# A decoder kernel on one core: in products by seven, the cast of the second sums is queued behind ScalarE's copies of the first group's banks

## The chip, the core and the metric

The kernel runs on one core of a Trainium2 chip. Five engines work side by side, each on its own queue in order: TensorE (PE, with its weight loads shown apart as PEld) multiplies matrices into PSUM, VectorE (DVE) and ScalarE (ACT) do elementwise work, GpSimd (POOL) here mostly issues transfers, SyncE (SP) issues the loads of weights. They wait for each other through semaphores. The metric is the device time of one execution in microseconds (us), as the median of several runs. A profiled execution also gives a span, from the first to the last instruction.

## The reference

A decoder trunk of two layers over 512 tokens of width 1024, in float32. Each layer is a SwiGLU FFN at half weight, a mixer (gated linear attention in the first layer, stick-breaking attention in the second), and a second FFN at half weight, each behind an RMSNorm. So four FFNs run:

```python
D_MODEL = 1024; SEQ = 512; DEPTH = 2; D_FF = 2816

def swiglu(h, w_gate, w_up, w_down):
    return (jax.nn.silu(h @ w_gate) * (h @ w_up)) @ w_down

for i in range(DEPTH):
    x = x + 0.5 * swiglu(rmsnorm(x, ffn1_norm[i]), ffn1_w_gate[i], ffn1_w_up[i], ffn1_w_down[i])
    h = rmsnorm(x, mix_norm[i])
    y = gla_mixer(h, ...) if i % N_MIXERS == 0 else sb_mixer(h, ...)
    x = x + y
    x = x + 0.5 * swiglu(rmsnorm(x, ffn2_norm[i]), ffn2_w_gate[i], ffn2_w_up[i], ffn2_w_down[i])
return rmsnorm(x, final_norm)
```

## The kernel before

**Precision.** Every float32 matrix is cut into two parts in a reduced format: `h` is a cast of it (ScalarE, line 138 for weights, 838 for activations) and `l` is what the cast lost (VectorE, lines 139 and 839: the original minus the cast). A product takes three matmuls: high by high, low by high, high by low. So for each piece of weights ScalarE makes `wh`, then VectorE makes `wl`, and only then can TensorE run all three.

**Products by seven.** Most FFN products are computed as a 2 by 2 block product with seven block products in place of eight, in the manner of Winograd and Strassen. A 1024 by 256 chunk of gate or up weights is cut into four blocks; `sums_12` makes the first two sums of blocks (tile `s12`, VectorE, lines 718 and 719), `sums_34` the second two (tile `s34`, lines 724 and 725). The rows of the trace call both tiles `s`. The work is two entries of a queue called the feed:

- `body_1` (line 750): four groups of 12 matmuls. The first writes bank `w` (from block a11). ScalarE then copies `w` to bank `z` (line 761), because both the later groups on `w` and the one on `z` go on from it. The second writes `q` (from `s12`); ScalarE copies it out (765). The third adds to `w` (from `s12`) and so may not begin before the copy at 761 has read `w`; ScalarE copies the result out (769). The fourth adds to `z` (from a2), read by a silu (743) or a VectorE product (746).
- `body_2` (line 776): three groups, on `w` (from `s34`), `q` (from `s34`) and `w` (from a2). The first of them may not begin before `w` was copied at 769. ScalarE copies `w` to `u3` (783), VectorE adds (784, 789), and for gate chunks three silus (743) follow.

The down product of two groups in each FFN does the same in halves (`seven_down`, line 358; matmuls at line 394): the same seven groups, each for two values of m, with two copies to `z` (412) in `body_1`, and with VectorE's additions into the residual x (line 400) in place of the copies at 765 and 769. There `body_2` adds to `w` too, and so it may not begin before the addition at line 400 has read `w`. Its sums are made at lines 378, 379, 385 and 386, and its `u3` is copied at 439.

**What sets the order.** `Feed.start` (line 146) is called when an entry begins. It calls `split` (the casts and subtractions, line 122) for this entry and the ones behind it, three entries at most and as long as no more than four tiles of 1024 columns are cut, so the casts of coming entries are in the program before the matmuls of this one. A scheduler then orders each engine's queue by the program's order and by priority; `ahead()` (line 192) raises the priority of a block. On the chip each queue runs in that order. TensorE's order is that of the program.

**Buffers.** `wh` and `wl` of 1024 columns have four buffers each, those of 512 columns one each; the sums share four.

**Stages of an FFN.** Chunks of 256 columns run in six groups. The first two chunks of gate use ordinary products; then gate and up chunks by seven alternate, with down products between them. Where two pairs of entries by seven stand directly behind one another, `body_2` of the one is followed by `body_1` of the next.

Of the kernel before, what the change touches and what calls it, by code (L numbers as in the profile page):

```python
# [10 lines left out]
F32 = mybir.dt.float32  # L11
F32R = mybir.dt.float32r
# [28 lines left out]
def pair(t):  # L41

    return t.rearrange("p (two n) -> p two n", two=2)
# [3 lines left out]
def decoder(ctx: ExitStack, tc: tile.TileContext, a: dict, out: bass.AP):  # L47
# [60 lines left out]
    class Entry:  # L108
# [3 lines left out]

        def __init__(self, units, body):
            self.units, self.body, self.W, self.views = units, body, None, None

        def view(self):

# [1 line left out]
                self.views = [view(ch.load()) for ch, view, _, _ in self.units]  # L119
            return self.views  # L120

        def split(self):
            if self.W is None:
                self.W = []
                for r, (_, _, n, m) in zip(self.view(), self.units):
                    few = n * m < 1024
                    if few:

                        h, l = (
                            st["few"].tile([P, n * m], F32R, tag="v" + t, bufs=1, name="w" + t) for t in "hl"  # L130
                        )
                    else:
                        h, l = (wp.tile([P, n * m], F32R, tag="w" + t, bufs=4, name="w" + t) for t in "hl")
                    h, l = (t.rearrange("p (n m) -> p n m", m=m) for t in (h, l))
                    pieces = r if isinstance(r, tuple) else (r,)
                    for i, part in enumerate(pieces):
                        k = slice(i * n // len(pieces), (i + 1) * n // len(pieces))
                        st["cut"] = nc.scalar.copy(h[:, k], part).ins  # L138
                        nc.vector.tensor_tensor(out=l[:, k], in0=part, in1=h[:, k].bitcast(F32), op=ALU.subtract)  # L139
                    self.W.append((h, l))  # L140

    class Feed:
        def __init__(self):
# [2 lines left out]
        def start(self):  # L146
            i = self.pos
            self.pos += 1
            used = 0
            for e in self.q[i : i + 3]:  # L150
                used += sum(n * m >= 1024 for _, _, n, m in e.units)
                if used > 4:
                    break
                e.split()
            for e in self.q[i : i + 4]:
                e.view()
            for e in self.q[i : i + 6]:
                for u in e.units:
                    u[0].load()
            e = self.q[i]  # L160
            return e.body(e.W)
# [196 lines left out]
    def seven_down(pool, w, r0, hs, part):  # L358

        H = T // 2
        lower, upper = (
            Chunk(w[r0 : r0 + 4 * P, c : c + 256].rearrange("(f p) c -> p f c", p=P), 4, 256)
            for c in (part * 256, 512 + part * 256)
        )
        lower.few = upper.few = True
        v = {}

        def halves():  # L370

            lo, up = (c.load().rearrange("p (c two) d -> p two c d", two=2) for c in (lower, upper))
            return lo[:, 0], lo[:, 1], up[:, 0], up[:, 1]

        def sums_12(_):
            a11, _, a21, a22 = halves()
            s = v["s12"] = pool().tile([P, 4, 256], F32, tag="s", bufs=4, name="s12")
            nc.vector.tensor_tensor(out=s[:, 0:2], in0=a21, in1=a22, op=ALU.add)
            nc.vector.tensor_tensor(out=s[:, 2:4], in0=s[:, 0:2], in1=a11, op=ALU.subtract)
            return s  # L380

        def sums_34(_):
            a11, a12, a21, _ = halves()
            s = pool().tile([P, 4, 256], F32, tag="s", bufs=4, name="s34")
            nc.vector.tensor_tensor(out=s[:, 0:2], in0=a11, in1=a21, op=ALU.subtract)
            nc.vector.tensor_tensor(out=s[:, 2:4], in0=a12, in1=v["s12"][:, 2:4], op=ALU.subtract)
            return s

        def prod(ps, w, k0, m, b, first):
            for c in range(2):  # L390
                bh, bl = (turns(t) for t in hs[c][b])
                wh, wl = (t[:, k0 + c, m * P : (m + 1) * P] for t in w)
                for n, (l_, r_) in enumerate(((wh, bh), (wl, bh), (wh, bl))):
                    st["pe"] = nc.tensor.matmul(  # L394
                        ps, l_, r_, start=first and c + n == 0, stop=c == 1 and n == 2, skip_group_check=True
                    ).ins

        def add(m, up, col, ps):
            x = pair(xs[part * 2 + m + 4 * up][:, col * H : col * H + H])
            nc.vector.scalar_tensor_tensor(out=x, in0=ps, scalar=0.5, in1=x, op0=ALU.mult, op1=ALU.add)  # L400

        def body_1(W):
            a11, s, v["a2"] = W
            ws, zs, qs = [], [], []
            for m in range(2):
                ws.append(psum("ps_w")[:, 0:H])
                prod(ws[m], a11, 0, m, "b11", True)
            for m in range(2):


                zs.append(psum("ps_z")[:, 0:H])
                nc.scalar.copy(zs[m], ws[m])
            yield

            ps = psum("ps_q")
            for m in range(2):
                qs.append(ps[:, m * H : (m + 1) * H])
                prod(qs[m], s, 0, m, "t1", m == 0)
            for m in range(2):
                add(m, 1, 1, flat(qs[m]))  # L420
            yield
            for m in range(2):
                prod(ws[m], s, 2, m, "t2", False)
                add(m, 0, 1, flat(ws[m]))
            yield
            for m in range(2):
                prod(zs[m], v["a2"], 0, m, "b21", False)
                add(m, 0, 0, flat(zs[m]))
            v["w"], v["q"] = ws, qs
            yield  # L430

        def body_2(W):
            (s,) = W
            ws, qs = v["w"], v["q"]

            u3 = pool().tile([P, 2, H], F32, tag="c", bufs=1, name="u3")
            for m in range(2):
                prod(ws[m], s, 0, m, "t3", False)
                nc.scalar.copy(pair(u3[:, m]), flat(ws[m]))
                add(m, 1, 1, pair(u3[:, m]))  # L440
            yield
            for m in range(2):
                prod(qs[m], s, 2, m, "b22", False)
            for m in range(2):
                add(m, 0, 1, flat(qs[m]))
            yield
            for m in range(2):
                prod(ws[m], v["a2"], 2, m, "t4", False)
                add(m, 1, 0, flat(ws[m]))
            yield  # L450

        units = [(lower, lambda t: halves()[0], 2, 256), (lower, sums_12, 4, 256), (lower, lambda t: halves()[1::2], 4, 256)]
        feed.q.append(Entry(units, body_1))
        feed.q.append(Entry([(lower, sums_34, 4, 256)], body_2))

    def back_tok(w, r0, nf, hs, done):

# [159 lines left out]
    class FFN:  # L617
# [90 lines left out]
        def seven(self, ch, group=None):  # L708
# [41 lines left out]
            def body_1(W):  # L750


                a11, s, a2 = W
                v["a2"] = a2
                v["w"], v["q"] = psum("ps_w"), psum("ps_q")
                z = psum("ps_z")[:, 0:H]
                w, q = (v[n][:, 0:H] for n in "wq")
                o0, o1 = v["o"] = [self.tp.tile([P, T], F32, tag="t", name=n) for n in ("o0", "o1")]
                prod(w, a11, 0, half(0, 0))
                with ahead():  # L760
                    nc.scalar.copy(z, w)  # L761
                yield
                prod(q, s, 0, lambda j: self.t_half(0, j))
                with ahead():
                    nc.scalar.copy(pair(o1[:, H:T]), flat(q))
                yield
                prod(w, s, 4, lambda j: self.t_half(1, j), first=False)
                with ahead():
                    nc.scalar.copy(pair(o0[:, H:T]), flat(w))
                yield  # L770
                prod(z, a2, 0, half(4, 0), first=False)
                with ahead():
                    gate(o0, 0, flat(z))
                yield
# [44 lines left out]
            units = [(ch, lambda t: t[:, 0:4, 0:P], 4, P), (ch, sums_12, KD, P), (ch, lambda t: t[:, 4:8], 4, 256)]  # L819
            feed.q.append(Entry(units, body_1))  # L820
            feed.q.append(Entry([(ch, sums_34, KD, P)], body_2))

        def t_half(self, i, j):

# [57 lines left out]
        def evac_u(self, ps, group):  # L882
            t = self.tp.tile([P, T], F32, tag="t", name="t")
            if not self.normed:
                nc.vector.tensor_tensor(out=pair(t), in0=flat(ps), in1=pair(st["R"]), op=ALU.mult)
            nc.vector.tensor_tensor(
                out=pair(t), in0=flat(ps) if self.normed else pair(t), in1=pair(self.gates.pop(0)), op=ALU.mult
            )
            self.close(t, group)

        def close(self, t, group):
            h = self.hp.tile([P, T], F32R, tag="hh", name="hh")
# [1043 lines left out]
```

## Time and profile before

| | |
|---|---|
| median of 3 runs | 1779.5 us (1779.32 to 1780.22) |
| the profiled execution's own time | 1778.36 us |
| its span | 1776.4 us |
| granted TensorE clock over the span | 0.999 |
| PE busy | 1755.4 us, 99% of the span |
| DVE busy | 1509.6 us, 85% |
| ACT busy | 1079.6 us, 61% |
| matmuls at line 733 and 394 (products by seven), one group of 12 | 1.34 us without a wait |

The profile lists busy time by engine, groups of instructions with their mean time, and who waited for whom. In rows of the timeline the first number is the start in us from the span's beginning, the second the duration in us (of the whole merged row); what stands in brackets is the idle time of that engine before the row, and what ended it. Instructions on one engine overlap a little at their ends, so the distance from one start to the next is what a queue pays.

### The profile page before, as it was taken

What the parts mean: (1) busy time and instruction counts of PE and PEld (TensorE: products, weight loads), DVE (VectorE), ACT (ScalarE), POOL (GpSimd) and SP (SyncE); (2) the same over time, 40 slices, a digit from 0 to 9 for tenths busy, and PEclk for the clock granted to TensorE, in tenths of its full rate; (3) what the DMA queues carried; (4) which work ended last, traced back from release to release, by engine and by line L of the source; (5) the groups of instructions that cost most, each with busy time, mean ns of one, the idle gap of its engine ahead of it and who ended that gap; (6) DMA issues with size and microseconds to landing.
All of it is one profiled execution on the core that took longest, in us unless ns stands there. A gap on an engine that the chain in (4) does not pass through costs nothing.

```text
span 1776.4 us, 31377 instructions
## 1 busy us (share of the span) xinstructions
PE 1755.4 (99%) x12714; PEld 1630.6 (92%) x12714; DVE 1509.6 (85%) x2474; ACT 1079.6 (61%) x1883; POOL 55.6 (3%) x77
## 2 busy tenths in 40 slices
PE   9999999999999999999999999999999999999998
PEld 8999999889888899999889999999888888999997
DVE  8999797786888989888798988967898679997986
ACT  7556556554655566555655555655888755565564
POOL 0000000200000000000000000010000000000000
PEclk9999999999999999999999999999999999999999
DMA  5543435422123433444434344342212234434441
GB/s 167 154 120 119 125 102 148 113 66 73 54 90 100 121 117 120 119 120 125 129 95 133 102 125 126 118 120 83 84 48 72 72 95 131 126 104 123 120 138 52
DMA packets 186388, 193.14 MB, mean 109 GB/s; under 512 B 4930, under 2 KB 171124, under 8 KB 186244
## 3 DMA queue, kind: packets, MB, share of 16 engines
q1 hardware_dynamic: 177760, 175.91, 31.7%
q0 software_dynamic: 8240, 14.95, 4.6%
q8 instruction: 99, 1.62, 0.4%
q14 instruction: 45, 0.37, 0.1%
q10 hardware_dynamic: 244, 0.29, 0.0%
HBM read 175.17 MB, written 2.10 MB: 100 GB/s over the span
## 4 chain that ended last, share of the span: by engine, by line
PE 60%; DVE 30%; ACT 5%; issue 3%; DMA 2%; SPq 0%; DVEq 0%; ACTq 0%
PE ps_w L733 13%; PE ps_d L80 12%; DVE wl L139 9%; PE ps_f L80 7%; PE ps_q L733 6%; PE ps_t L80 4%; PE ps_z L733 3%; PE ps_b L80 3%; PE ps_w L394 3%; ACT wh L138 2%; DVE x L400 2%; DVE hl L839 1%; PE ps_q L394 1%; DVE ts L848 1%; PE ps_z L1424 1%
## 5 line engine op out<-in xcount | busy, mean ns | idle before, releaser
L139 DVE TENSOR_TENSOR wl<-raw,wh 128x1024 fp32r<-128x1024 f32 x241 | 255.5, 1061 | 59.4 <-ACT wh L138 58.8
L138 ACT CAST wh<-raw 128x1024 fp32r<-128x1024 f32 x241 | 221.6, 920 | 77.8 <-PE ps_f L80 22.6
L139 DVE TENSOR_TENSOR wl<-s,wh 128x1024 fp32r<-128x1024 f32 x176 | 214.6, 1219 | 50.7 <-ACT wh L138 50.7
L733 PE MATMUL ps_w<-th,wh 128*128 128x256 f32 x864 | 239.4, 277 | 6.3 <-ACT ps_z L761 6.3
L733 PE MATMUL ps_w<-th,wl 128*128 128x256 f32 x864 | 237.6, 275 | 0.0
L733 PE MATMUL ps_w<-tl,wh 128*128 128x256 f32 x864 | 237.6, 275 | 0.0
L138 ACT CAST wh<-s 128x1024 fp32r<-128x1024 f32 x176 | 184.1, 1046 | 69.6 <-DVE s L719 19.4
L733 PEld LDWEIGHTS ps_w<-th,wh 128*128 128x128 f32 x864 | 165.8, 192 | 9.5 <-ACT ps_z L761 9.4
L80 PE MATMUL ps_f<-xh,wh 128*128 128x512 f32 x432 | 166.4, 386 | 0.0
L733 PEld LDWEIGHTS ps_w<-tl,wh 128*128 128x128 f32 x864 | 165.9, 192 | 0.0
L733 PEld LDWEIGHTS ps_w<-th,wl 128*128 128x128 f32 x864 | 165.8, 192 | 0.0
L80 PE MATMUL ps_f<-xh,wl 128*128 128x512 f32 x432 | 164.2, 380 | 0.5 <-DVE wl L139 0.5
L80 PE MATMUL ps_f<-xl,wh 128*128 128x512 f32 x432 | 163.9, 379 | 0.0
L80 PE MATMUL ps_d<-hl,wh 128*128 128x512 f32 x416 | 158.0, 380 | 1.7 <-DVE hl L839 1.7
L80 PE MATMUL ps_d<-hh,wh 128*128 128x512 f32 x416 | 158.0, 380 | 0.5 <-ACT hh L838 0.5
L80 PE MATMUL ps_d<-hh,wl 128*128 128x512 f32 x416 | 157.7, 379 | 0.0
L139 DVE TENSOR_TENSOR wl<-rawd,wh 128x1024 fp32r<-128x1024 f32 (+1 forms) x100 | 96.1, 964 | 15.8 <-ACT wh L138 15.1
L138 ACT CAST wh<-rawd 128x1024 fp32r<-128x1024 f32 (+1 forms) x100 | 82.9, 845 | 39.4 <-PE ps_d L80 25.6
L345 POOL DMA_DIRECT2D x<-d x53 | 45.8, 888 | 1510.1 <-ACT d L344 832.2
L80 PEld LDWEIGHTS ps_f<-xl,wh 128*128 128x128 f32 x432 | 81.6, 189 | 11.5
L80 PEld LDWEIGHTS ps_f<-xh,wl 128*128 128x128 f32 x432 | 81.7, 189 | 11.3 <-DVE wl L139 0.9
L80 PEld LDWEIGHTS ps_f<-xh,wh 128*128 128x128 f32 x432 | 81.7, 189 | 10.8
(355 smaller groups left out, 5331.4 us busy)
## 6 DMA issues: line engine op xcount, KB each, us to landing
raw<-in_ffn_w_gate_dram SPq DMA_DIRECT2D x43, 1024.0 KB, 5.4
raw<-in_ffn_w_up_dram SPq DMA_DIRECT2D x43, 1024.0 KB, 5.4
rawd<-in_ffn_w_down_dram SPq DMA_DIRECT2D x84, 512.0 KB, 3.8
x<-d POOLq DMA_DIRECT2D x53, 256.0 KB, 4.6
raw<-in_gla_w_in_dram SPq DMA_DIRECT2D x12, 1024.0 KB, 5.4
raw<-in_sb_w_in_dram SPq DMA_DIRECT2D x16, 512.0 KB, 3.7
raw<-in_gla_w_out_dram SPq DMA_DIRECT2D x4, 1024.0 KB, 5.1
raw<-in_sb_w_in_dram SPq DMA_DIRECT2D x4, 1024.0 KB, 5.2
```

The lines of the kernel that those rows point to most:

```text
L80: st["pe"] = nc.tensor.matmul(ps, l, r, start=first, stop=last).ins
L138: st["cut"] = nc.scalar.copy(h[:, k], part).ins
L139: nc.vector.tensor_tensor(out=l[:, k], in0=part, in1=h[:, k].bitcast(F32), op=ALU.subtract)
L345: nc.gpsimd.dma_start(xs[k], d, accum_op=ALU.add)
L394: st["pe"] = nc.tensor.matmul(ps, l_, r_, start=first and c + n == 0, stop=c == 1 and n == 2, skip_group_check=True).ins
L400: nc.vector.scalar_tensor_tensor(out=x, in0=ps, scalar=0.5, in1=x, op0=ALU.mult, op1=ALU.add)
L733: st["pe"] = nc.tensor.matmul(o, l_, r_, start=first and j + n == 0, stop=j == 3 and n == 2, skip_group_check=True).ins
L839: nc.vector.tensor_tensor(out=l, in0=t, in1=h.bitcast(F32), op=ALU.subtract)
L848: nc.vector.tensor_tensor(out=o, in0=p, in1=q, op=ALU.subtract)
L1424: nc.tensor.matmul(o_, l_, r_, start=first, stop=last, skip_group_check=True)
```

## The change

`split` takes an instruction to be queued behind, and its body becomes a function `parts` that cuts one piece. ScalarE's cast is traced under `issue_after`, which puts it behind the given instruction on ScalarE's queue. Both makers of products by seven mark the second entry of a pair; `Feed.start` stops before a second entry whose first group's copy isn't in the program yet if the entry two places ahead of it is a second entry too (so for pairs directly behind one another). That entry is cut in `body_1` of its pair instead, behind the copy of bank `w` to `z` (behind the later of the two copies for the halves of down). The copies at 412 are put under `ahead()`, and so are the product and the cut in `evac_u`.

```diff
@@ class Entry
             self.units, self.body, self.W, self.views = units, body, None, None
+            self.second, self.v = False, None
...
-        def split(self):
+        def split(self, after=None):
             if self.W is None:
                 self.W = []
                 for r, (_, _, n, m) in zip(self.view(), self.units):
...
+                    self.W.append(self.parts(r, n, m, after))
+
+        def parts(self, r, n, m, after):
...
+            for i, part in enumerate(pieces):
+                k = slice(i * n // len(pieces), (i + 1) * n // len(pieces))
+                with tc.issue_after(after) if after is not None else ExitStack():
+                    nc.scalar.copy(h[:, k], part)
+                nc.vector.tensor_tensor(out=l[:, k], in0=part, in1=h[:, k].bitcast(F32), op=ALU.subtract)
+            return h, l
@@ Feed.start
-            for e in self.q[i : i + 3]:
+            for n, e in enumerate(self.q[i : i + 3]):
+                if e.v is not None and "copied" not in e.v and self.q[i + n - 2].second:
+                    break
                 used += sum(n * m >= 1024 for _, _, n, m in e.units)
                 if used > 4:
                     break
@@ seven_down, body_1
-                nc.scalar.copy(zs[m], ws[m])
+                with ahead():
+                    v["copied"] = nc.scalar.copy(zs[m], ws[m]).ins
+            v["second"].split(v["copied"])
             yield
@@ seven_down and FFN.seven, at their ends
+        v["second"] = feed.q[-1]
+        feed.q[-1].second, feed.q[-1].v = True, v
@@ FFN.seven, body_1
                 with ahead():
-                    nc.scalar.copy(z, w)
+                    v["copied"] = nc.scalar.copy(z, w).ins
+                v["second"].split(v["copied"])
                 yield
@@ FFN.evac_u
-            nc.vector.tensor_tensor(
-                out=pair(t), in0=flat(ps) if self.normed else pair(t), in1=pair(self.gates.pop(0)), op=ALU.mult
-            )
-            self.close(t, group)
+            with ahead():
+                nc.vector.tensor_tensor(
+                    out=pair(t), in0=flat(ps) if self.normed else pair(t), in1=pair(self.gates.pop(0)), op=ALU.mult
+                )
+                self.close(t, group)
```

TensorE's and SyncE's rows stand in the same order in both kernels; ScalarE's and VectorE's move in the same four stretches of each of the four FFNs, and one load of GpSimd moves by two places. The rows below are of the first FFN. Names with a number are tiles of sums and outputs (numbers differ a little between the kernels); the changed file's lines lie 5 to 15 further down, so that 143 is the cast of weights (138 before), 144 its subtraction (139), 772 the copy to `z` (761), 777 and 781 the copies of `q` and `w` (765, 769), 754 the silu (743), 420 the copy in the halves of down (412), 407 the addition into x (400), 852 and 853 the cut of activations (838, 839).

The first place is ScalarE where a gate pair ends and an up pair begins. Before (`s_1348` are the second sums of the up pair, `s_1426` the first sums of the pair behind it):

```order
L743 ACTIVATE o_1355<-o_1355 128x256
L138 CAST wh<-s_1348 128x1024
L743 ACTIVATE o_1354<-o_1354 128x256
L743 ACTIVATE o_1355<-ps_w 128x256
L138 CAST wh<-s_1426 128x1024
L761 COPY ps_z<-ps_w 128x256
L138 CAST wh<-rawd 128x512
L765 COPY o_1481<-ps_q 128x256
L769 COPY o_1480<-ps_w 128x256
```

The same place in the changed kernel (`s_1422` is the `s_1426` of before):

```order
L754 ACTIVATE o_1355<-o_1355 128x256
L754 ACTIVATE o_1354<-o_1354 128x256
L754 ACTIVATE o_1355<-ps_w 128x256
L772 COPY ps_z<-ps_w 128x256
L143 CAST wh<-s_1348 128x1024
L143 CAST wh<-rawd 128x512
L777 COPY o_1477<-ps_q 128x256
L143 CAST wh<-s_1422 128x1024
L781 COPY o_1476<-ps_w 128x256
```

Both casts of sums that stood before the copy to `z` stand behind it now, and the second of them stands between the copies of `q` and `w`.

The second place is VectorE a little later, at the halves of down (`s_1474`, now `s_1470`, are its second sums, x_85 and so on parts of the residual). Before:

```order
L139 TENSOR_TENSOR wl<-s_1474,wh 128x1024
L746 TENSOR_TENSOR o_1481<-ps_w,o_1355 128x256
L839 TENSOR_TENSOR hl<-o_1480,hh 128x512
L139 TENSOR_TENSOR wl<-s_1552,wh 128x1024
L839 TENSOR_TENSOR hl<-o_1481,hh 128x512
L400 SCALAR_TENSOR_TENSOR x_85<-ps_q,x_85 128x256
L400 SCALAR_TENSOR_TENSOR x_86<-ps_q,x_86 128x256
L400 SCALAR_TENSOR_TENSOR x_81<-ps_w,x_81 128x256
```

In the changed kernel:

```order
L729 TENSOR_TENSOR s_1684<-raw 128x512
L757 TENSOR_TENSOR o_1477<-ps_w,o_1355 128x256
L853 TENSOR_TENSOR hl<-o_1476,hh 128x512
L730 TENSOR_TENSOR s_1684<-s_1684,raw 128x512
L853 TENSOR_TENSOR hl<-o_1477,hh 128x512
L144 TENSOR_TENSOR wl<-s_1470,wh 128x1024
L407 SCALAR_TENSOR_TENSOR x_85<-ps_q,x_85 128x256
L407 SCALAR_TENSOR_TENSOR x_86<-ps_q,x_86 128x256
L407 SCALAR_TENSOR_TENSOR x_81<-ps_w,x_81 128x256
```

The subtraction for the second sums has moved directly in front of the additions into x, and later first sums (729, 730) have come in between.

The third place is ScalarE where the first up pair of group 1 ends and a gate pair begins (`nh`, `hh` are cuts of activations, `s_866`, now `s_862`, the gate pair's second sums). Before:

```order
L783 COPY u_956<-ps_w 128x256
L838 CAST nh<-o_874 128x256
L138 CAST wh<-s_866 128x1024
L138 CAST wh<-rawd 128x1024
L761 COPY ps_z<-ps_w 128x256
L838 CAST hh<-o_875 128x512
L838 CAST hh<-ts 128x512
L838 CAST nh<-ts 128x256
L765 COPY o_1019<-ps_q 128x256
```

In the changed kernel:

```order
L795 COPY u_952<-ps_w 128x256
L852 CAST nh<-o_870 128x256
L852 CAST nh<-ts 128x256
L852 CAST hh<-o_871 128x512
L852 CAST hh<-ts 128x512
L772 COPY ps_z<-ps_w 128x256
L852 CAST nh<-ts 128x256
L143 CAST wh<-s_862 128x1024
L777 COPY o_1011<-ps_q 128x256
L143 CAST wh<-rawd 128x1024
L781 COPY o_1010<-ps_w 128x256
```

Here the two weight casts have left the place before the copy to `z`, and three casts of activations have come to stand there.

More of the change, by code (lines that the diff above doesn't have):

```diff
@@ L125, in split @@
                 for r, (_, _, n, m) in zip(self.view(), self.units):
[L126 to L130, printed above, removed]
-                        )
[L132 to L140, printed above, removed]
+                    self.W.append(self.parts(r, n, m, after))
+        def parts(self, r, n, m, after):
+            few = n * m < 1024
+            if few:
+                h, l = (
+                    st["few"].tile([P, n * m], F32R, tag="v" + t, bufs=1, name="w" + t) for t in "hl"
+                )
+            else:
+                h, l = (wp.tile([P, n * m], F32R, tag="w" + t, bufs=4, name="w" + t) for t in "hl")
+            h, l = (t.rearrange("p (n m) -> p n m", m=m) for t in (h, l))
+            pieces = r if isinstance(r, tuple) else (r,)
+            for i, part in enumerate(pieces):
[4 more added lines that the diff above has]
+            return h, l
     class Feed:
@@ L821, in seven @@
             feed.q.append(Entry([(ch, sums_34, KD, P)], body_2))
+            v["second"] = feed.q[-1]
+            feed.q[-1].second, feed.q[-1].v = True, v
         def t_half(self, i, j):
@@ L885, in evac_u @@
                 nc.vector.tensor_tensor(out=pair(t), in0=flat(ps), in1=pair(st["R"]), op=ALU.mult)
[L886 to L889 removed]
+            with ahead():
+                nc.vector.tensor_tensor(
+                    out=pair(t), in0=flat(ps) if self.normed else pair(t), in1=pair(self.gates.pop(0)), op=ALU.mult
+                )
+                self.close(t, group)
         def close(self, t, group):
```

## The prediction

> **What bounds the kernel now.** I read the page's busy shares first, then the waits of TensorE, then the groups by line, and last the timeline around the longest and the commonest of those waits.
>
> ```profile
> PE 1755.4 (99%) x12714; PEld 1630.6 (92%) x12714; DVE 1509.6 (85%) x2474; ACT 1079.6 (61%) x1883; POOL 55.6 (3%) x77
> PE ps_w L733 <- ACT ps_z L761: 6.3, 16, 1.1
> PEld ps_w L733 <- ACT ps_z L761: 9.4, 16, 1.3
> PEld ps_w L394 <- ACT ps_z L412: 0.5, 1, 0.5
> ```
>
> TensorE is busy in 99% of the span, so only what it waits for can be won, and nearly half of that is one thing: the third group of a product by seven waits for ScalarE's copy to `z`, 16 times. The commonest form of it, on ScalarE and then on TensorE:
>
> ```profile
> 122.44 0.42 ACT L743 ACTIVATE o<-o 128x256 f32<-128x256 f32 x1 [1.84 <-DVE o L784]
> 122.77 1.03 ACT L138 CAST wh<-s 128x1024 fp32r<-128x1024 f32 x1
> 123.70 0.41 ACT L743 ACTIVATE o<-o 128x256 f32<-128x256 f32 x1
> 124.02 0.37 ACT L743 ACTIVATE o<-ps_w 128x256 f32<-128x256 f32 x1
> 124.28 1.05 ACT L138 CAST wh<-s 128x1024 fp32r<-128x1024 f32 x1
> 125.22 0.38 ACT L761 COPY ps_z<-ps_w 128x256 f32<-128x256 f32 x1
> 125.52 0.63 ACT L138 CAST wh<-rawd 128x512 fp32r<-128x512 f32 x1
> ...
> 125.11 0.28 PE L733 MATMUL ps_q<-th,wl 128*128 128x256 f32 x1
> 125.22 0.28 PE L733 MATMUL ps_q<-tl,wh 128*128 128x256 f32 x1
> 125.66 0.38 PE L733 MATMUL ps_w<-th,wh 128*128 128x256 f32 x1 [0.16 <-ACT ps_z L761]
> 125.87 0.28 PE L733 MATMUL ps_w<-th,wl 128*128 128x256 f32 x1
> ```
>
> Three silus of the pair that ends, late because VectorE's sums were late (1.84 us idle), share the queue with two casts of sums at 0.93 and 0.94 from start to start. So the copy starts at 125.22. TensorE steps at 0.11 us (0.112 over many, so 1.34 for a group of 12); the waiting matmul starts 0.44 behind the last, 0.33 too late, and its successor 0.21 behind it, another 0.10. A wait thus costs the visible delay plus 0.10 for starting again.
>
> **What the change removes.** In pairs directly behind one another both casts leave the place ahead of the copy. The first group on `w` ended where `q` began, 11 steps before 125.22, at 123.99; by the rows below a copy follows such an end by 0.2 to 0.25.
>
> ```profile
> 85.50 0.28 PE L733 MATMUL ps_q<-th,wh 128*128 128x256 f32 x1
> 85.75 0.36 ACT L761 COPY ps_z<-ps_w 128x256 f32<-128x256 f32 x1 [0.35 <-PE ps_w L733]
> 86.02 0.62 ACT L838 CAST hh<-o 128x512 fp32r<-128x512 f32 x1
> 86.54 0.62 ACT L838 CAST hh<-ts 128x512 fp32r<-128x512 f32 x1
> 121.99 0.42 DVE L784 TENSOR_TENSOR o<-u,o 128x256 f32<-128x256 f32 x1
> 122.92 0.42 DVE L789 TENSOR_TENSOR o<-ps_q,o 128x256 f32<-128x256 f32 x1
> ```
>
> The silus may start when VectorE is done, at 122.44 and 123.37, the third 0.32 later; so the copy starts at 124.2 and ends before 124.6, and TensorE wants it at 125.33. The wait here is gone. The order shows the same at every one of the 16, and at the one of line 412. A weight load lasts 0.192 (its group reads 192 ns) at a step of 0.112, so 0.08 of each wait hides under the last load:
>
> ```profile
> L733 PEld LDWEIGHTS ps_w<-th,wh 128*128 128x128 f32 x864 | 165.8, 192 | 9.5 <-ACT ps_z L761 9.4
> ```
>
> Removed: 9.4 + 16 x 0.08 = 10.7, and 0.5 + 0.1 = 0.6 at line 412, together **11.3 us**.
>
> [...]
>
> **What it gives back at the halves of down.** ScalarE's cast of the second sums now starts after the copy (0.30 from start to start at 125.22 and 125.52), at 124.5, and ends at 125.55. VectorE's subtraction for it stands at the same place in VectorE's queue as before, so VectorE, which began it at 123.86, waits until 125.6. These are the steps it then takes:
>
> ```profile
> 132.52 1.22 DVE L139 TENSOR_TENSOR wl<-s,wh 128x1024 fp32r<-128x1024 f32 x1
> 133.66 0.42 DVE L746 TENSOR_TENSOR o<-ps_w,o 128x256 f32<-128x256 f32 x1
> 133.99 0.68 DVE L839 TENSOR_TENSOR hl<-o,hh 128x512 fp32r<-128x512 f32 x1
> 134.59 1.22 DVE L139 TENSOR_TENSOR wl<-s,wh 128x1024 fp32r<-128x1024 f32 x1
> 135.72 0.68 DVE L839 TENSOR_TENSOR hl<-o,hh 128x512 fp32r<-128x512 f32 x1
> 136.33 0.75 DVE L400 SCALAR_TENSOR_TENSOR x<-ps_q,x 128x256 f32<-128x256 f32 x2
> 136.99 0.41 DVE L400 SCALAR_TENSOR_TENSOR x<-ps_w,x 128x256 f32<-128x256 f32 x1
> ...
> 137.82 0.28 PE L394 MATMUL ps_w<-nh,wh 128*128 128x256 f32 x1
> ```
>
> From start to start a subtraction of 1024 columns takes 1.14, an operation on 512 columns 0.60, one on 256 columns 0.33 to 0.34, two additions into x 0.66; one addition lasts 0.41. By the order there stand, from that subtraction to the end of the addition that `body_2` of the halves of down waits for, three of 1024 (3.42), nine of 512 (5.40), six of 256 (2.03), two additions from `q` (0.66) and one from `w` (0.41): 11.9 us, ending at 137.5. The third subtraction waits for its cast besides. That cast stands behind the second copy at line 412, which stands behind a cut `hh`; the sum for this cut ends at 133.6 by the same steps; 0.52 for the cut, 0.30 for the copy and 1.05 for the cast give 135.5, where VectorE arrives at 135.3. So 137.7. TensorE, with no wait, is there nine groups behind 125.33, at 125.33 + 9 x 1.34 = 137.39. In the run shown the addition ended at 137.40 and TensorE came at 137.82: 0.42 to spare, and now 0.35 short with the semaphore's 0.05, plus 0.10 for the restart. That is 0.45 of the 0.43 won. Three such places stand in each FFN (the pair behind each of them: 125, 241 and 270 us in the first), and the spacing inside is fixed by TensorE, so 12 x 0.45 = **5.4 us**. Bounds: none (if VectorE's steps run 3% faster), and 12 x 0.8 = 9.6 if the steps are 3% slower.
>
> **What it gives back elsewhere.** The copy at line 769 now stands behind the cast of the second sums (0.95), of 512 columns (0.52), the copy of `q` (0.27) and the cast of the next first sums (0.95); with the copy to `z` (0.27) and its own 0.37 it ends 3.33 behind the start of the copy to `z`. It must end 5.36 (four groups) behind the pair's start; the copy to `z` normally starts 1.34 + 0.2 behind it. The slack is 0.49, so nothing is lost where the silus are on time, as at 124.2. At the worst place they aren't:
>
> ```profile
> 74.64 0.42 DVE L789 TENSOR_TENSOR o<-ps_q,o 128x256 f32<-128x256 f32 x1
> 75.73 0.36 ACT L743 ACTIVATE o<-ps_w 128x256 f32<-128x256 f32 x1
> ...
> 76.01 0.28 PE L733 MATMUL ps_q<-tl,wh 128*128 128x256 f32 x1
> 77.36 0.38 PE L733 MATMUL ps_w<-th,wh 128*128 128x256 f32 x1 [1.07 <-ACT ps_z L761]
> ```
>
> VectorE ends at 75.06, two silus follow at 0.32 each, and the copy starts at 75.73, which leaves TensorE on time at 76.12 within 0.05 (1.2 won and 0.1). But the pair began at 76.12 - 2.68 = 73.44, the copy at 769 ends at 79.06, and TensorE wants it at 78.80: 0.3 lost. The next copy to `z` there has three cuts of activations ahead of it (third place of the order) where it had two casts that were done early. Counting from VectorE's sums at the steps above I get it 0.4 late, then 0.1 at its copy of `w`. With the restarts that is 1.1 of 1.3. This stretch had such a wait in two FFNs; in the other two it had none and loses some 0.1 to 0.2. Together 2 x 1.1 + 2 x 0.15 = **2.5 us**, between 1 and 4.
>
> **What costs nothing.** The order moves no row for `evac_u`: VectorE's order is the same there, and the priority changes nothing. Transfers keep their order; the load that moves on GpSimd's queue waits on nothing that TensorE needs soon. `wl` of the second sums must be there 0.11 behind the start of `body_2`: cast at 2.9, subtraction done at 4.1 behind the pair's start, 1.3 us of cover; without it each pair would lose what is missing. The instructions and their number stay the same.
>
> **The sum.** 11.3 - 5.4 - 2.5 = 3.4, and 0.2 for delays under 0.1 us that go with the removed waits: 3.6 us off the profiled execution's 1778.36 (span 1776.4, 2.0 around it), so 1774.8 (span 1772.8). The median of the runs shown, 1779.5, lies 1.1 above the profiled one: **1775.9 us**.
>
> **Rivals.**
>
> Clean gain: VectorE has its slack, nothing comes back at line 400 and little at 769. For it: 0.42 to spare there before, and VectorE's idle time. Against: the steps above. 11.3 - 1 = 10.3: 1769.2.
>
> No net change: the losses reach their upper bounds, 9.6 + 2.5 against 11.3: 1780, or 1778 to 1781 with one of them less. For it: the first stretch alone gives back nearly all it wins.
>
> Slower, VectorE as the bound: in the longest of these stretches VectorE has almost nothing left.
>
> ```profile
> 122.00:181.00 59.00, 58.39 (x516) 57.91 (x515) 56.49 (x97) 36.70 (x67) 0.00 (x0) 1.00 0.37 117
> 171.28 1.22 DVE L139 TENSOR_TENSOR wl<-s,wh 128x1024 fp32r<-128x1024 f32 x1 [1.09 <-ACT wh L138]
> ```
>
> Its subtraction of second sums now always waits for a cast that follows TensorE. In the first of these stretches that adds waits of about 1.6, 1.0 and 1.7 us to a queue that waited 2.2, so some 2 us, and, counted likewise, 1.7 in the one from 238 us. If the sums behind it are needed at once, TensorE pays these 3.7 us in each FFN, 14.8 in place of the 5.4: 11.3 - 14.8 - 2.5 = -6, so 1785.5. It decides once VectorE's work of a pair no longer ends within the pair's 9.38 us. Against: 56.49 of 59.00 includes the adds and sums that can be late without anyone waiting. [...]
>
> That the change doesn't do what it says: the order excludes it for the casts, and grants it for `evac_u`.
>
> **How the numbers follow.** Forecast (2 to 5.5 us gained) 0.55, clean gain 0.14, no net change 0.20, slower 0.11. About 0.2% (3.6 us) can be told from no change here: that is the middle of my forecast. Faster by more: 0.31 of the forecast's 0.55 and the clean gain, 0.45. Slower by more: VectorE as the bound, 0.11. Within: the rest, 0.44. The range from 1771 to 1781 takes in the bounds of the two losses one at a time, half of the way to the clean gain and the case of no change.
>
> **What would show it.** Right: the waits for line 761 (772 in the changed file) fall below 3 us; new waits of TensorE for VectorE's addition at line 400 (407), about 12 of them at 0.3 each; a few for the copy at 769 (781), all within 74 to 95 us and its like in the third FFN; VectorE's waits for the casts of sums grow. Wrong: the waits at 761 remain; none at 400, or waits for `wl` of the second sums; a total over 1781, which would mean that VectorE no longer keeps up.

## The result, and the profile after

| | before | changed |
|---|---|---|
| median of the runs, us | 1778.69 (14 runs, 1777.63 to 1780.22) | 1775.05 (14 runs, 1774.33 to 1776.63) |
| profiled execution, us | 1778.36 | 1776.0 |
| its span, us | 1776.4 | 1774.1 |
| TensorE's waits for the copy to `z` (PE / PEld), us | 6.3 / 9.4 | 0.2 / 0.6 |

The changed kernel takes 0.998 of the time before, with a 95% interval of 0.9973 to 0.9987: it is 3.6 us faster. The forecast was 1775.9.

First the changed kernel's page: the busy shares, and the groups that answer to those quoted of before.

```profile
PE 1756.3 (99%) x12714; PEld 1631.8 (92%) x12714; DVE 1505.5 (85%) x2474; ACT 1074.7 (61%) x1883; POOL 55.6 (3%) x77
L144 DVE TENSOR_TENSOR wl<-s,wh 128x1024 fp32r<-128x1024 f32 x176 | 215.2, 1223 | 82.6 <-ACT wh L143 80.2
L744 PEld LDWEIGHTS ps_w<-th,wh 128*128 128x128 f32 x864 | 165.8, 192 | 1.8 <-ACT o L781 0.7
```

The subtraction's row on the page before:

```profile
L139 DVE TENSOR_TENSOR wl<-s,wh 128x1024 fp32r<-128x1024 f32 x176 | 214.6, 1219 | 50.7 <-ACT wh L138 50.7
```

The work is the same in number and in length (1223 ns a subtraction after 1219, 192 ns a weight load). What changed is the idle time behind the bar: the loads of the groups on `w` wait 1.8 us where they waited 9.5, and VectorE waits 80.2 us for the casts of sums, where before it waited 50.7. Most of those 30 us cost nothing, since VectorE is not the bound; the part of them that reaches TensorE shows in the next rows.

Next, TensorE's waits in the changed kernel (line waited at, releaser: us in total, times, longest), first of the matmuls, then of the weight loads.

```profile
PE ps_w L401 <- ACT wh L143: 2.6, 9, 0.3
...
PE ps_w L401 <- DVE x L407: 0.8, 3, 0.3
...
PE ps_w L744 <- ACT ps_z L772: 0.2, 1, 0.2
PEld ps_w L401 <- issue: 5.3, 12, 0.5
...
PEld ps_w L744 <- ACT o L781: 0.7, 3, 0.2
PEld ps_w L744 <- ACT ps_z L772: 0.6, 2, 0.4
```

None of the 16 waits of before is left. The two short ones at line 772 (761 before) stand at 86.35 and 955.04 us, at copies that made nobody wait before the change. New are also 12 waits at line 401, the first matmul of `body_2` in the halves of down, at some 0.3 each on the matmul and 0.44 on its load. The profile names VectorE's addition at 407 for three of them and ScalarE's cast at 143 for nine.

The timeline at the commonest place of before shows the part that was won, on ScalarE and then on TensorE:

```profile
122.21 0.42 ACT L754 ACTIVATE o<-o 128x256 f32<-128x256 f32 x1 [1.90 <-DVE o L796]
123.14 0.42 ACT L754 ACTIVATE o<-o 128x256 f32<-128x256 f32 x1 [0.52 <-DVE o L801]
123.47 0.36 ACT L754 ACTIVATE o<-ps_w 128x256 f32<-128x256 f32 x1
123.91 0.36 ACT L772 COPY ps_z<-ps_w 128x256 f32<-128x256 f32 x1
124.17 1.05 ACT L143 CAST wh<-s 128x1024 fp32r<-128x1024 f32 x1
...
124.93 0.28 PE L744 MATMUL ps_q<-tl,wh 128*128 128x256 f32 x1
125.05 0.28 PE L744 MATMUL ps_w<-th,wh 128*128 128x256 f32 x1
```

The silus start when VectorE is done, with no cast between them; the copy ends at 124.27, the third group begins at 125.05, one step of 0.12 behind the last matmul. The same pair then pays at the halves of down. VectorE, ScalarE and TensorE there:

```profile
135.19 1.22 DVE L144 TENSOR_TENSOR wl<-s,wh 128x1024 fp32r<-128x1024 f32 x1 [0.15 <-ACT wh L143]
136.33 0.75 DVE L407 SCALAR_TENSOR_TENSOR x<-ps_q,x 128x256 f32<-128x256 f32 x2
137.00 0.75 DVE L407 SCALAR_TENSOR_TENSOR x<-ps_w,x 128x256 f32<-128x256 f32 x2
...
134.09 1.06 ACT L143 CAST wh<-s 128x1024 fp32r<-128x1024 f32 x1
...
136.99 0.28 PE L401 MATMUL ps_z<-hl,wh 128*128 128x256 f32 x1
137.56 0.35 PE L401 MATMUL ps_w<-nh,wh 128*128 128x256 f32 x1 [0.29 <-ACT wh L143]
137.74 0.28 PE L401 MATMUL ps_w<-nh,wl 128*128 128x256 f32 x1
```

The first of the two additions from `w` ends at about 137.41 (137.00 and 0.41 for one), and TensorE, which would have come at 137.10, starts at 137.56. The cast that the profile names had ended at 135.15. By the starts, 12 such places are late by 0.43 to 0.45 each.

### The profile page after: what moved, and what is told of

It reads as the page before. It is cut to its first block, busy times and chain, and to the rows that moved or that the text cites. A ratio compares the mean times of both kernels' runs of the same rounds, so it can differ in the third digit from the quotient of the medians.

```text
span 1774.1 us, 31336 instructions
## 1 busy us (share of the span) xinstructions
PE 1756.3 (99%) x12714; PEld 1631.8 (92%) x12714; DVE 1505.5 (85%) x2474; ACT 1074.7 (61%) x1883; POOL 55.6 (3%) x77
## 4 chain that ended last, share of the span: by engine, by line
PE 67%; DVE 21%; ACT 7%; issue 3%; DMA 1%; DVEq 0%; ACTq 0%; SPq 0%
PE ps_w L744 17%; PE ps_d L80 13%; PE ps_q L744 8%; PE ps_f L80 7%; DVE wl L144 6%; PE ps_t L80 4%; PE ps_z L744 4%; ACT wh L143 4%; PE ps_w L401 3%; PE ps_b L80 3%; PE ps_q L401 1%; DVE ts L862 1%; PE ps_z L1439 1%; DMA raw<-in_ffn_w_gate_dram 1%; DVE xn L846 1%
## 5 line engine op out<-in xcount | busy, mean ns | idle before, releaser
L144 DVE TENSOR_TENSOR wl<-s,wh 128x1024 fp32r<-128x1024 f32 x176 | 215.2, 1223 | 82.6 <-ACT wh L143 80.2
L80 PE MATMUL ps_f<-xh,wh 128*128 128x512 f32 x432 | 166.4, 386 | 0.0
L80 PE MATMUL ps_f<-xh,wl 128*128 128x512 f32 x432 | 164.2, 380 | 0.5 <-DVE wl L144 0.5
L80 PE MATMUL ps_f<-xl,wh 128*128 128x512 f32 x432 | 163.9, 379 | 0.0
L80 PE MATMUL ps_d<-hl,wh 128*128 128x512 f32 x416 | 158.0, 380 | 1.7 <-DVE hl L853 1.7
L80 PE MATMUL ps_d<-hh,wh 128*128 128x512 f32 x416 | 158.0, 380 | 0.5 <-ACT hh L852 0.5
L80 PE MATMUL ps_d<-hh,wl 128*128 128x512 f32 x416 | 157.7, 379 | 0.0
L80 PEld LDWEIGHTS ps_f<-xl,wh 128*128 128x128 f32 x432 | 81.6, 189 | 11.5
L80 PEld LDWEIGHTS ps_f<-xh,wl 128*128 128x128 f32 x432 | 81.7, 189 | 11.3 <-DVE wl L144 0.9
L80 PEld LDWEIGHTS ps_f<-xh,wh 128*128 128x128 f32 x432 | 81.7, 189 | 10.8
```

The costliest lines, as they stand in the source:

```text
L80: st["pe"] = nc.tensor.matmul(ps, l, r, start=first, stop=last).ins
```

## The experiments

Two theories were set against each other first. Theory A: at the halves TensorE waits for VectorE's addition, which the late cast has pushed back. Theory B: it waits for the cast itself, as the profile says in nine cases of twelve.

### Only the chunks keep the deferral

In the changed kernel, the halves of down cut their second sums as early as before:

```diff
@@ seven_down, body_1
-            v["second"].split(v["copied"])
+            v["second"].split()
@@ seven_down, at its end
-        feed.q[-1].second, feed.q[-1].v = True, v
+        feed.q[-1].second = True
```

> The second sums of the halves of down are cut early again, as before the change (their cast is not queued behind the copies at line 412); those of the chunks stay queued behind their copy. Theory A (the 12 new waits of TensorE at line 401 are for VectorE's addition at 407, and VectorE's chain of about 12 us from the late cast sets them): the chain loses two sums of 0.60 and 0.15 us of waiting for the cast and gains one subtraction of 1.14, so it ends 0.2 earlier; the waits shrink from 0.44 to about 0.2 and the time falls by 2.5 us against the changed kernel, to about 1772.5. Rival B (TensorE waits for ScalarE's cast of the second sums itself, which the waits name as releaser in 9 of 12 cases): the cast is some 4 us earlier, the waits vanish, 12 x 0.54 = 6.5 us less, 1768.5.

Measured: 1780.21 us (11 runs, 1779.67 to 1781.22), before 1779.4, ratio 1.0004 (0.9995 to 1.0013): no gain at all. Both theories missed the time. TensorE's waits in this kernel:

```profile
PE ps_w L401 <- ACT ps_z L420: 3.1, 8, 0.7
...
PE ps_w L744 <- DVE wl L144: 1.5, 3, 1.2
```

The 12 waits at the first matmul of `body_2` are gone but for the restarts. B expected that, where A expected 0.2 us each to be left; but the addition, too, ends earlier here, 24.10 us behind the start of its stretch in place of 24.42. New waits stand in other places. The timeline of ScalarE and TensorE at one of the eight at line 420:

```profile
170.35 1.04 ACT L143 CAST wh<-s 128x1024 fp32r<-128x1024 f32 x1
...
172.12 1.05 ACT L143 CAST wh<-rawd 128x1024 fp32r<-128x1024 f32 x1 [0.16 <-DMA rawd<-in_ffn_w_down_dram]
173.08 0.64 ACT L420 COPY ps_z<-ps_w 128x256 f32<-128x256 f32 x2
...
173.50 0.38 PE L401 MATMUL ps_w<-hh,wh 128*128 128x256 f32 x1 [0.22 <-ACT ps_z L420]
```

Two casts stand ahead of the halves' own copies, and the second even waits for a load. The kernel before at the same place:

```profile
171.73 1.03 ACT L138 CAST wh<-rawd 128x1024 fp32r<-128x1024 f32 x1
172.67 0.64 ACT L412 COPY ps_z<-ps_w 128x256 f32<-128x256 f32 x2
...
173.38 0.28 PE L394 MATMUL ps_w<-hh,wh 128*128 128x256 f32 x1
```

So the early cut did bring back ScalarE's order ahead of these copies. What differs is the timing. Counted from the starts of this stretch (113.06 and 113.28), TensorE wants the copy at the same time, 60.06 and 60.11, and the copy comes 0.63 later. In the third stretches it is TensorE that comes earlier, at 49.83 in place of 50.78, since it has lost less on the way. In the kernel before, seven of these eight copies were in time by 0.15 to 0.35 us and one was late; here all eight are late by 0.34 to 0.88 by the starts, 5.2 us with their restarts; in the changed kernel they end 1.2 us ahead of TensorE (at this place they start at 171.02, and TensorE comes at 172.60). The deferral in the halves thus costs the waits at 401 and keeps these eight away. The waits for `wl` in a `body_2` of a chunk (three on the matmuls, four by the starts, 2.7 us with restarts) have another cause in the same kernel; the longest, on VectorE and TensorE:

```profile
1017.18 0.69 DVE L729 TENSOR_TENSOR s<-raw 128x512 f32<-128x512 f32 x1 [1.97 <-DMA raw<-in_ffn_w_gate_dram]
1017.78 1.22 DVE L144 TENSOR_TENSOR wl<-s,wh 128x1024 fp32r<-128x1024 f32 x1
...
1019.06 0.38 PE L744 MATMUL ps_w<-th,wl 128*128 128x256 f32 x1 [1.17 <-DVE wl L144]
```

A sum that waits 1.97 us for its load stands ahead of the subtraction in VectorE's queue. So this run moved more than the part that it was to undo, and does not say which theory holds.

### Only the halves keep the deferral

```diff
@@ FFN.seven, body_1
-                v["second"].split(v["copied"])
@@ FFN.seven, at its end
-            feed.q[-1].second, feed.q[-1].v = True, v
+            feed.q[-1].second = True
```

> Only the halves of down are changed: their second sums are queued behind the copies at 412; the chunks' second sums are cut early as before. Both theories: the 16 waits at the copy to z (9.4 us on PEld) are back. Theory A: VectorE's chain to the addition at 407 starts 1.7 us earlier than in the changed kernel, so there is no wait at line 401, or a marginal one, and the time is that of before less about 0.5 us: 1778. Rival B: the cast stands behind the copies at 412 as in the changed kernel, so the waits at 401 remain, 12 to 16 x 0.54, and the time is slower than before by about 6 us: 1785.

Measured: 1777.98 us (10 runs, 1776.87 to 1780.01), ratio 0.9992 (0.9983 to 1.0001). TensorE's waits:

```profile
PE ps_w L744 <- ACT ps_z L772: 4.3, 14, 0.9
...
PEld ps_w L744 <- ACT ps_z L772: 7.4, 16, 1.1
PEld ps_w L401 <- issue: 1.2, 4, 0.5
```

Most of the waits at 772 are back and only four of the twelve places at 401 are late. The time fits A's 1778, and B's 1785 is out. The reason is not quite the one that A gave. VectorE does come to the halves' subtraction early, but there it waits 0.78 us for the deferred cast at the first place (136.92), so the addition comes only some 0.1 us earlier in the stretch than in the changed kernel. TensorE comes 0.44 later (139.39 behind a start at 114.84, against 137.10 behind 112.99), because it has lost that time at the copy to `z`. Where it lost nothing there, as ahead of 1712.06 us, the start at 401 is 0.46 late, as in the changed kernel. Since TensorE's arrival moved too, this run alone does not rule out that the cast releases TensorE.

### One operation more for VectorE

To measure the chain, the changed kernel got one unused addition of 512 columns on VectorE ahead of the additions into x:

```diff
@@ seven_down, body_1
+            junk = pool().tile([P, 2, H], F32, tag="c", bufs=1, name="junk")
+            part_ = v["a2"][0][:, 0:2].bitcast(F32)
+            extra = nc.vector.tensor_tensor(out=junk, in0=part_, in1=part_, op=ALU.add).ins
             for m in range(2):
-                add(m, 1, 1, flat(qs[m]))
+                with tc.issue_after(extra):
+                    add(m, 1, 1, flat(qs[m]))
```

(and likewise the addition from `w`).

> The changed kernel with one more VectorE operation on 512 columns (0.60 us, result unused) in the chain ahead of the additions at 407 in the halves of down; the cast stands where it stands in the changed kernel. Theory A: the addition comes 0.60 less the 0.15 that VectorE now waits for the cast, 0.45 later, so the 12 waits grow from 0.44 to 0.9, plus up to four new ones at the second halves: 5.4 to 7 us slower than the changed kernel, about 1781. Rival B: the cast is not moved, waits at 401 stay at 0.44, the time stays at 1775 within 1 us.

Measured: 1779.95 us (10 runs, 1779.37 to 1781.86), ratio 1.0003 (0.9994 to 1.0012), so 4.9 us more than the changed kernel's 1775.05, a little under A's 5.4 to 7. The two were timed in different sessions; each against the kernel before of its own session, 0.55 slower and 3.64 faster, they are 4.2 apart. TensorE's waits:

```profile
PE ps_w L401 <- DVE x L407: 7.8, 12, 0.7
...
PEld ps_w L401 <- ACT wh L143: 9.7, 12, 0.8
```

The same twelve places, each now 0.81 late by the starts where it was 0.45, and the matmul's waits are all put down to the addition. Twelve times 0.36 is 4.3 us, which accounts for the difference. An operation on VectorE that has nothing to do with ScalarE's cast moves TensorE: the addition decides, as in A. The growth is 0.36 a place and not 0.60, the step of such an operation in the prediction. In the changed kernel the subtraction at 135.19 starts 0.84 behind the row before it (134.35), where such a step takes 0.60, because it waits for the cast; the added operation first fills these 0.24.

### ScalarE copies the bank, VectorE adds from the copy

If the addition is late only because it reads the bank, then a copy of the bank by ScalarE releases it. The changed kernel with that alone:

```diff
@@ seven_down, body_1
+            u2 = pool().tile([P, T], F32, tag="t", name="u2").rearrange("p (a b) -> p a b", a=2)
             for m in range(2):
                 prod(ws[m], s, 2, m, "t2", False)
-                add(m, 0, 1, flat(ws[m]))
+                with ahead():
+                    nc.scalar.copy(pair(u2[:, m]), flat(ws[m]))
+                add(m, 0, 1, pair(u2[:, m]))
```

> The changed kernel, but in the halves of down ScalarE copies bank w to SBUF after the third group and VectorE adds from that copy, so that TensorE need not wait for VectorE's addition there; the copies stand behind the casts of the second sums and of the next first sums, ahead of the cast of the next a2 block. Theory A: the copy ends at about 136.9 us in the first FFN where the addition ended at 137.41 and TensorE comes at 137.10, so the 12 waits go: 6.5 us less, 1768.5, less what the 32 more copies of 0.37 us cost on ScalarE (nothing if they fit in its idle time, up to 2 us if copies to z come late). Rival B: the cast is not moved, the waits stay, 1775.

Measured: 1770.42 us (5 runs, 1769.95 to 1772.93), ratio 0.9952 (0.994 to 0.9964): 4.6 us less than the changed kernel's 1775.05. Against the kernel before of its own session it wins 9.0 us between the medians, where the changed kernel won 3.6, so the copy is worth some 5 us. It lies within A's 1768.5 to 1770.5 and is the fastest kernel of this study. The timeline at the same place, on VectorE, ScalarE and TensorE:

```profile
135.07 1.23 DVE L144 TENSOR_TENSOR wl<-s,wh 128x1024 fp32r<-128x1024 f32 x1
...
136.88 0.75 DVE L407 SCALAR_TENSOR_TENSOR x<-u,x 128x256 f32<-128x256 f32 x2
...
133.98 1.06 ACT L143 CAST wh<-s 128x1024 fp32r<-128x1024 f32 x1
...
136.40 0.64 ACT L435 COPY u<-ps_w 128x256 f32<-128x256 f32 x2
...
136.88 0.28 PE L401 MATMUL ps_z<-hl,wh 128*128 128x256 f32 x1
136.99 0.28 PE L401 MATMUL ps_w<-nh,wh 128*128 128x256 f32 x1
```

Cast, subtraction and additions stand within 0.12 us of where they stood in the changed kernel; the bank is free when the first copy ends (before 136.77), and TensorE goes on without a gap (0.11 from start to start). No wait at 401 appears among this kernel's waits; a few restarts are left. With the cast unmoved and the wait gone, B is out.

### The copy alone, on the kernel before

The same copy without the change, to see whether it is a gain of its own:

> The kernel before, with nothing but ScalarE's copy of the bank w in the halves of down (the edit that took the changed kernel from 1775 to 1770). Theory A (the copy pays only because the deferred cast had made VectorE's addition late; before the change that addition had 0.42 us to spare): no more than 1 us from the kernel before, so a ratio of 0.9995 to 1.0005, and TensorE's waits for the copy to z stay (PEld about 9.4 us, 16 waits). Rival C (the copy frees VectorE or the bank w whatever the order of casts, and is a gain of its own that has nothing to do with the change): about 5 us faster, ratio 0.997.

Measured: 1779.3 us (11 runs, 1778.2 to 1781.4), before 1779.68, ratio 1.0 (0.9991 to 1.0009). The wait of its weight loads for the copy to `z`:

```profile
PEld ps_w L736 <- ACT ps_z L764: 10.1, 17, 1.2
```

It is as long as before (9.4 there), and nothing was won. So the copy is worth some 5 us behind the change and nothing without it: the wait that it removes is one that the change made.

### Without the part in `evac_u`

```diff
@@ FFN.evac_u
-            with ahead():
-                nc.vector.tensor_tensor(...)
-                self.close(t, group)
+            nc.vector.tensor_tensor(...)
+            self.close(t, group)
```

> The changed kernel without the raised priority in evac_u, the one part of the change that was said to cost and win nothing because no row moves. If so: the changed kernel's time within 1 us (1774 to 1776.5), and the waits for hl at the end of the FFNs unchanged at 1.7 us in 2. If the priority matters in a way the order of rows does not show, the time moves by more than that.

Measured: 1776.05 us (10 runs, 1774.83 to 1777.94), before 1779.68, ratio 0.9982 (0.9973 to 0.9991). That is the changed kernel's ratio within its interval, and the rows of every engine stand in the same order in the two kernels. TensorE's waits:

```profile
PE ps_w L401 <- ACT wh L143: 2.9, 10, 0.3
...
PE ps_d L80 <- DVE hl L853: 1.7, 2, 0.8
```

The wait for `hl` at the end of an FFN is 1.7 in 2 with the raised priority and without it, as before the change (`PE ps_d L80 <- DVE hl L839: 1.7, 2, 0.8` there). This run serves as a second execution of the changed order too.

## Why the prediction was right, point by point

For each stretch of products by seven, the length from TensorE's first matmul to the first one behind it can be compared with before; what the starts show late is then set against it. The sums over the four FFNs, in us, less than before (the first stretch of an FFN is that from 64 us, the second from 113, the third from 229, and their like):

```
                                   first   second   third   sum
late starts before, with restarts   2.64     3.72    4.81   11.17
won by the changed kernel           1.18     0.50    1.05    2.73
  the same without evac_u's part    1.43     1.52    1.03    3.98
  the same with ScalarE's copy      1.25     2.56    4.79    8.60
```

**Removed, 11.3 us.** By the starts the 16 waits cost 8.98 us, the one at line 412 0.46, and the 17 restarts 0.10 each: 11.1. All of it went; the late starts at 86.35 (0.34) and 955.04 us (0.22) are new ones and belong to what was given back. The third stretches of the kernel with ScalarE's copy won 4.79 against 4.81, which agrees with 0.10 for each restart; without the restarts the sum would be 4.0. The removal needed both halves of the change, which the prediction did not say: with the chunks alone deferred, eight waits at 420 appeared (5.2 us), and with those for `wl` nothing was won.

**Given back at the halves, 5.4 us.** Mechanism, places and number were right: 12, behind the pairs named. Each start is 0.45 late and its successor 0.07 more (0.18 from 137.56 to 137.74, at a step of 0.11), 0.52 together, so 6.2 us for twelve. The prediction had 0.45. VectorE's chain came out as forecast: the addition ended 0.31 us after TensorE would have come (137.41 and 137.10; forecast 137.7 and 137.39), with 0.24 of waiting for the cast where 0.2 was forecast. The piece that was too small is the way from the end of the addition to the matmul: 0.15 us pass (137.41 to 137.56, and the same at the other eleven) where 0.05 was put in, which is what passes behind ScalarE's copy in the rows of before (125.60 to 125.66). The restart, taken as 0.10, was 0.07. Taking the waits away with ScalarE's copy returns a little less, since that kernel pays some restarts of its own: in the third stretches, with two such places each, 4.79 - 1.05 = 3.74 us, 0.47 a place.

**Given back elsewhere, 2.5 us.** Too large, and in part in the wrong place. The rest of what was won and lost again is 11.17 - 6.2 - 2.73 = 2.2 us in the changed run, and 11.17 - 6.2 - 3.98 = 1.0 in the one without `evac_u`'s part. The first stretches, to which the prediction gave all of it, lost 2.64 - 1.18 = 1.5 in the changed run. The second lost 1.1 beside the halves' waits, and the third won 0.4 more than their late starts, in delays under 0.1 us each, for which the prediction had 0.2 in all. Of the first stretch, the copy to `z` behind three cuts is 0.34 late in the first FFN and 0.22 in the third, for which 0.4 was said. But at the copy of `w` (line 781), for which 0.3 was said at 79 us, almost nothing is lost:

```profile
78.78 0.38 ACT L781 COPY o<-ps_w 128x256 f32<-128x256 f32 x1
...
79.05 0.28 PE L744 MATMUL ps_z<-nl,wh 128*128 128x256 f32 x1
79.21 0.38 PE L744 MATMUL ps_w<-th,wh 128*128 128x256 f32 x1
```

The copy ends at 79.16 where 79.06 was forecast. TensorE however arrives at 79.16 and not at 78.80: its whole stretch began 0.37 later than in the profiled run of before (64.43 after 64.06), while the VectorE steps that lead to the copy came only 0.13 later (74.77 after 74.64). That delay of TensorE comes from the first 10 us of the execution (the last section; the same matmul starts at 9.84 here and at 9.47 before), and not from the change. In the runs whose stretch began at 64.16 to 64.24 (early halves, one operation more, the copy on ScalarE) the wait is there, 0.2 at 79 us by the starts. The step that failed is the claim that waits for the copy at 781 lie "all within 74 to 95 us and its like in the third FFN". The three in the changed run lie at 1034, 1584 and 1594 us, in the second stretches, 0.2 each, and the second run of the same order has none of them. The slack of 0.49 that the prediction gave this copy in the other pairs was in truth nearly nothing: in the second run the starts there are on time, but each of the four FFNs has one restart 0.10 late at this copy (166.05, 710.85, 1034.85 and 1593.42 us). Why one execution of the same order pays 0.2 more at some of them stays open.

**At no cost.** No row moved for `evac_u`, the time without it is the same, and `wl` of the second sums was always in time in the changed kernel. VectorE did not become the bound: its wait for the casts of sums grew by 30 us and its busy time stayed at 85%.

**The sum.** 11.2 - 6.2 - 2.2 = 2.7 in one execution of this order, 4.0 in the other, and 3.6 between the medians. The forecast said 3.6, with the halves 0.8 too small and the rest 0.3 to 1.5 too large. The mechanism was right in its main parts; that the sum agrees to 0.1 us is luck, since two errors of opposite sign cancel and single executions of the order differ by more than 1 us. The loads' 9.4 us, from which the forecast was added up, were real time: with them gone 8.6 us are won once the halves' waits are out of the way too.

**The rivals.** The clean gain (1769.2) is what happens when the halves' waits are taken away by other means, 1770.42; the change alone does not get there. No net change and VectorE as the bound are out by the interval. The length of VectorE's chain comes close to deciding between them: with one operation of 512 columns more the gain is gone (1779.95).

## What to carry to other kernels

When a wait is removed by moving work behind it on one engine, follow that work through every engine to the next buffer that the bound engine needs: here a cast moved by 1.7 us on ScalarE came back as 0.5 us a place on TensorE, through a subtraction that stands in VectorE's fixed order. Ask the same of the next wait of the bound engine: with the chunks alone deferred, eight copies in the halves came late, of which seven had been just in time, and cost 5.2 us. Where the last link of the chain is an operation that TensorE needs only for the bank it frees, let an engine with time to spare copy the bank out; here ScalarE, busy 61% of the span, did it, and the same copy was worth nothing on the kernel before (ratio 1.0) and 4.6 us once the chain was the bound. The releaser that a profile names can be the wrong one, so set its end beside the start that it is said to explain.

## What the runs showed of the hardware

**The named releaser.** Nine of the twelve waits at line 401 were put down to a cast that had ended more than 2 us earlier (135.15 against 137.56). The kernel with the longer VectorE chain, which moved these starts and not the cast, has its matmuls' waits under the addition and its loads' waits under the cast, at the same twelve places.

**TensorE's steps at the start vary between executions.** The first stretch of products by seven began at 64.06 to 64.50 us in seven profiled runs and at 65.76 in one, that of the deferral in the halves only. The difference arises in the first 10 us, in equal instructions. First the kernel before, then that run:

```profile
4.82 1.10 PE L1718 MATMUL ps_x<-ident,x 128*128 128x128 f32 x8
7.14 0.38 PE L1727 MATMUL ps_f<-xh,wh 128*128 128x512 f32 x1
7.36 0.38 PE L1727 MATMUL ps_f<-xh,wl 128*128 128x512 f32 x1
```

```profile
4.65 1.97 PE L1732 MATMUL ps_x<-ident,x 128*128 128x128 f32 x8
7.55 0.63 PE L1741 MATMUL ps_f<-xh,wh 128*128 128x512 f32 x1
7.98 0.63 PE L1741 MATMUL ps_f<-xh,wl 128*128 128x512 f32 x1
```

The steps from start to start are 0.22 in the one and 0.43 in the other, though the windows of the profile give a granted clock of 1.00 for both. TensorE ran at half its pace until about 10 us there. In the kernel before, the eight matmuls at 4.82 took 1.10 us where the same eight took 1.97 in that run, and the steps are 0.22 from 7.14 on. In the eight profiled runs these eight matmuls take from 1.10 to 1.97 us; what ends the slow steps, and why not at the same time in each execution, no run shows. The 1.7 us that the slow steps cost here (65.76 after 64.06) are near half of the whole gain under study. So a difference of 1.7 us between two single executions of this kernel need not come from the change, unless the first 10 us are taken out.
